# Four edits to a decoder layer on one Trainium2 core: an earlier sample softmax, an on-chip sample output, sooner sample queries and another order of heads in a projection

## The chip, the core and the metric

The kernel runs on one core of a Trainium2 chip. The metric is the device time of one execution in microseconds (us); lower is better. TensorE (PE in the profile) does the matrix products and the transposes, VectorE (DVE) and ScalarE (ACT) do the element-wise work, GpSimd (POOL) a little of it, and SyncE (SP) mostly issues DMA transfers; ACT and POOL issue some transfers too. Each engine works through its own list of instructions in order. The order is fixed when the program is built, so an instruction that waits holds back everything behind it on its engine.

## The reference, cut to what matters

One layer is computed for 1,024 prompt tokens and for 8 sample sequences of 4 new tokens each, 1,056 columns in all, with a model width of 1,024:

```python
SEQ = 1024; DEC_BATCH = 8; DEC_SEQ = 4; PAST_LEN = 512; N_MEM = 256; CA_HEADS = 4
# 1. one input projection -> [S5 diagonal state-space group | differential attention], one output projection
#    prompt: attention over the prompt; sample: over a paged cache of 512 tokens and its own 4
# 2. cross-attention, 4 heads of width 256, into 256 memory tokens
#    (prompt: keys from mem_prompt; sample: cache_mem_k, cache_mem_v, one set for each sequence)
# 3. gated FFN with a causal depthwise convolution
out = g * jax.nn.sigmoid(g @ p['ssm_glu_w'])          # gate behind the state-space scan
s = jnp.einsum('bqhid,bkhid->bhiqk', q, k) * ATTN_HEAD_DIM ** -0.5
pr = jax.nn.softmax(s + bias, axis=-1)
a = pr[:, :, 0] - lam * pr[:, :, 1]                   # differential attention
```

All of it is fp32. Each fp32 product is three products of a high and a low part, so that one tile of a projection takes three matmuls (`mm3`, lines 187 to 189: high by high, low by high, high by low).

## The kernel before

The columns are cut into three blocks, 0 to 383, 384 to 767 and 768 to 1055. The last 32 columns of the third block are the samples. A projection of one 128-wide output tile over one block is 24 matmuls, 8 contraction tiles `k` by three, of 384 or 288 columns. Python generators write the program; a driver takes turns between them by costs that they yield, and a scheduler then settles each engine's order; `tc.high_priority()` ranks what stands in it ahead of other ready work. Four places matter.

**Behind the scan.** The last quarter of the state-space scan (`yp`, `tp__`, gelu on `ge_a` and `yt`) runs beside the sample attention: `soft(s)` turns scores into `Pm` and `Sw`, `values(s)` multiplies pages `V` of the cache by them into `Op`, and the normalized result `os__5850` is transposed into `qsT` by `turn_samples`. The gate products (`zp`, with `th` for the tanh) follow block by block, and the attention result of the prompt comes back from memory as `ms<-mixT`, is split into `Mh` and `Ml` by `load_part`, and feeds the output projection `pp<-Mh`. Sixteen loads of the residual stream (`Xh`, `Xl`) of 528 KB each stand in SP's queue there too; the memory that they fill is free only when the sample attention is done with it.

**Cross-attention.** For each of four heads, three generators run side by side: `wq_head` projects the queries (`pp<-Xh`), `ca_head` does the prompt's attention (scores `S`, probabilities `P`, transposes `pts`, split `Ph`/`Pl`, output `po`), and `sample_keys` does the sample scores. The last loads eight tiles `kt` of 256 KB for a head, through two buffers, has TensorE transpose each (`pt<-ident,kt`), ACT copy it to `KT`, and after every four tiles adds 8 matmuls to `Ssm`. `sample_query` (transposed scale `pb`, then `Qc`) has to come first. All of `pt`, `pts`, `pq` (query norms) and `pb` share two PSUM buffers.

**Output projection of cross-attention.** `wo_stage` takes the heads' outputs from memory (`ms<-coT`, k = 0 to 5) or, for head 3, from SBUF (`coh`, `col`, k = 6 and 7). It does the first four output tiles of blocks 0 and 1, then waits in program order for `sample_values` (16 pages `vt` of 512 KB through three buffers, `Op<-vt`, then `os_`, its transposes `pt<-os_`, and the splits of the sample columns), then does the rest.

**Order of loads.** SP issues `kt`, `ms`, `V` and the weights; POOL issues `vt`.

Of the kernel before, what the change touches and what calls it, by code (L numbers as in the profile page):

```python
# [20 lines left out]
SEQ = 1024  # L21
# [48 lines left out]
def hymba_step(ctx: ExitStack, tc: tile.TileContext, A: dict, O: dict, upto=99, dbg=None):  # L70
# [120 lines left out]
    def fl(a):  # L191
        return a.rearrange("p a b -> p (a b)")
# [1162 lines left out]
    def turn_samples(s, os_, po):  # L1355
        nc.tensor.transpose(po[:, :128], os_, ident)
        nc.vector.tensor_scalar(
            out=qsT[:, :, 16 * s:16 * s + 16].rearrange("p h (b t) -> p b h t", t=DS),
            in0=po[:, :128].rearrange("p (b x) -> p b x", b=4)[:, :, 0:16].rearrange("p b (h t) -> p b h t", t=DS),
            scalar1=gsub, scalar2=None, op0=ALU.mult)  # L1360

    def sample_attention(sa):
# [45 lines left out]

        def soft(s):
            Sp = Sps[s]  # L1410
            Pm = sa.tile([128, PAST + NS], F32, tag="big", name="Pm", bufs=KTB)
            mx = sa.tile([128, 1], F32, tag="mxs", name="mxs")
            sm_ = sa.tile([128, 1], F32, tag="sms", name="sms")
            mx2 = sa.tile([128, 2], F32, tag="mx2", name="mx2")
            c = PAST + NS * s
            nc.vector.tensor_tensor_reduce(out=Pm[:, PAST:], in0=newS[:, s], in1=tabS[:, c:c + NS], scale=-1.0,
                                           scalar=3.0e38, op0=ALU.add, op1=ALU.min, accum_out=mx2[:, 0:1])
            nc.vector.tensor_tensor_reduce(out=Pm[:, :PAST], in0=Sp, in1=tabS[:, :PAST], scale=-1.0,
                                           scalar=3.0e38, op0=ALU.add, op1=ALU.min, accum_out=mx2[:, 1:2])
            tt(out=mx, in0=mx2[:, 0:1], in1=mx2[:, 1:2], op=ALU.min)  # L1420
            nc.scalar.activation(out=Pm, in_=Pm, func=AF.Exp, scale=-1.0, bias=mx, accum_out=sm_)
            nc.vector.reciprocal(out=sm_, in_=sm_)
            tt(out=sm_, in0=sm_, in1=sgn, op=ALU.mult)
            Sw = sa.tile([128, 128], F32, tag="Sw", name="Sw")
            nc.vector.tensor_scalar(out=Sw, in0=fl(Sel), scalar1=sm_, scalar2=None, op0=ALU.mult)
            yield Y[2]
            aT = sa.tile([128, NPG + 1, 128], F32, tag="aT", name="aT")
            pt = tp("pt", "td")
            for pg in range(NPG):
                nc.tensor.matmul(pt[:, 128 * pg:128 * pg + 128], lhsT=Pm[:, 128 * pg:128 * pg + 128], rhs=Sw,  # L1430
                                 start=True, stop=True)
            nc.scalar.copy(fl(aT[:, :NPG]), pt)
            pn = tp("pn", "td")
            nc.tensor.matmul(pn[:NS, :128], lhsT=Pm[:, PAST:], rhs=Sw, start=True, stop=True)
            nc.scalar.copy(aT[:NS, NPG], pn[:NS, :128])
            yield 1100
            aTs.append(aT)
# [99 lines left out]
                                op1=ALU.add)  # L1537
        rsqrt(pl, r, v, 9)

    def load_part(pl, Mh, Ml, src, row, k, b):  # L1540
        t0, n = TB[b]
        ms = pl.tile([128, 384], F32, tag="xn", name="ms", bufs=4)
        nc.sync.dma_start(out=ms[:, :n], in_=src[row:row + 128, t0:t0 + n])
        split(Mh[k][:, t0:t0 + n], Ml[k][:, t0:t0 + n], ms[:, :n])
# [9 lines left out]
    with ExitStack() as p4:  # L1554
# [47 lines left out]
        for b in range(3):  # L1602
            for d in range(4):
                if (d, b) not in early:
                    gate(d, b, (0, 1, 2, 3))
            if b == 1:
                turn_samples(1, tail['os'], ps.tile([128, 512], F32, tag="pj", name="po"))
                nc.gpsimd.dma_start(out=mixT[:, SEQ:].rearrange("(h p) t -> p h t", p=128), in_=qsT)
            for h in range(NH):
                load_part(wx, Mh, Ml, mixT, 128 * h, 4 + h, b)  # L1610
        for d in range(KD):
            for i, X in enumerate((Xh, Xl)):
                nc.sync.dma_start(out=r32(X[:, d]), in_=xT_d[i][128 * d:128 * d + 128, :])
# [17 lines left out]
    with ExitStack() as p5:  # L1631
# [7 lines left out]
        Qc = ca.tile([128, 2, NB, 32], F32, name="Qc", bufs=1)  # L1639
        Ssm = ps_q.tile([128, NMEM], F32, name="Ssm")  # L1640
        hq = {}
        queries = set()
        scaled, late = set(), []
        BORD = [2, 0, 1]
        CKB = 1
# [5 lines left out]
        def wq_head(h):  # L1651
# [15 lines left out]
            nc.vector.memset(ssq, 1.0)  # L1667
            rs = ca.tile([128, 9], F32, tag="crs", name="crs")
            hq[h] = (kh, kl, vh, vl, cqt, rs)
            for oi, bi in enumerate(BORD):  # L1670
                t0, n = TB[bi]
                while h >= 1 and blocks[h - 1] < oi:
                    yield None
                ch = ca.tile([128, 2, 384], F32R, tag="ch", name="ch", bufs=4)
                cl = ca.tile([128, 2, 384], F32R, tag="cl", name="cl", bufs=4)
                sqs = []
                for z in range(2):
                    pp = ps_j.tile([128, 384], F32, tag="pj", name="pp")
                    for k in range(KD):
                        mm3(pp[:, :n], w[z][0][:, k], w[z][1][:, k], Xh[:, k, t0:t0 + n], Xl[:, k, t0:t0 + n],  # L1680
                            k == 0, k == KD - 1)
                        if k % 2:
                            yield 6 * n / 2.4
                    if late:
                        late.pop()()
                        yield 350
                    split_g(ch[:, z, :n], cl[:, z, :n], pp[:, :n], GT[:, 124 + z:125 + z])
                    sq = ca.tile([128, 384], F32, tag="csq", name="csq")
                    nc.scalar.activation(out=sq[:, :n], in_=pp[:, :n], func=AF.Square)
                    sqs.append(sq)  # L1690
                tt(out=sqs[0][:, :n], in0=sqs[0][:, :n], in1=sqs[1][:, :n], op=ALU.add)

                cqt[bi] = (ch, cl)
                late.append(lambda bi=bi, t0=t0, sq=sqs[0]: query_scale(h, bi, t0, sq, ssq, rs))
# [26 lines left out]
        def sample_query(h, cqt, rs):  # L1721
# [7 lines left out]
            for z in range(2):  # L1729
                for s in range(2):  # L1730
# [1 line left out]
                    tt(out=Qc[:, z, 4 * s:4 * s + 4, c:c + 4],  # L1732
                       in0=cs_[:, z, 16 * s:16 * s + 16].rearrange("p (b t) -> p b t", t=DS),
                       in1=pb[:, 16 * s:16 * s + 16].rearrange("p (b t) -> p b t", t=DS), op=ALU.mult)
            queries.add(h)

        def ca_head(h):
            while h not in hq:
# [28 lines left out]
            for oi, bi in enumerate(BORD):  # L1767
# [12 lines left out]
                    split(Ph[:, :, 128 * j:128 * j + 128], Pl[:, :, 128 * j:128 * j + 128], pts)  # L1780
                    yield 220
                yield CA[1]
                if bi == 2:
                    sample_query(h, cqt, rs)
                for z in range(2):
                    po = ps_o.tile([128, 384], F32, tag="po", name="po")
                    for c in range(2):
# [12 lines left out]
                    yield 6 * nq / 2.4  # L1800

        def sample_keys(h):
            while h not in queries:
                yield None
            for s in range(2):
                KT = ca.tile([128, 4, 2, NMEM], F32, tag="KT", name="KT", bufs=CKB)
                for b4 in range(4):
# [53 lines left out]
    with ExitStack() as p7:  # L1861
# [59 lines left out]
        def wo_stage():  # L1921
# [5 lines left out]
            def part(d, b):  # L1927
                t0, n = TB[b]
                pp = ps.tile([128, 384], F32, tag="pj", name="pp")
                for k in range(KD):  # L1930
                    mm3(pp[:, :n], w[d][0][:, k], w[d][1][:, k], Mh[k][:, t0:t0 + n], Ml[k][:, t0:t0 + n],
                        k == 0, k == KD - 1)
                    if k == 3:
                        yield 12 * n / 2.4
                update_x(wx, pp[:, :n], d, t0, n, d == 0)
                yield 12 * n / 2.4
# [197 lines left out]
```

## Time and profile before

| | |
|---|---|
| median of 3 runs | 1818.07 us (1816.73 to 1818.88) |
| the profiled execution | 1823.91 us, span of its instructions 1822.0 us |
| TensorE busy | 1713.6 us, 94% of the span |
| VectorE, ScalarE, GpSimd busy | 60%, 33%, 28% |
| granted TensorE clock, mean | 0.961 |

The profiled execution took 5.84 us more than the median and 1.91 us more than its own span. TensorE is the engine that is nearly always busy; its granted clock is told as a share of full speed, 1.00 at 2.4 GHz and 0.50 at 1.2 GHz. From about 1100 us on, in the FFN, TensorE shows no idle time at clock 1.00, so what can change lies before.

### The profile page before, as it was taken

The numbers are of one execution on the slowest core, as the hardware profiler recorded it, in microseconds if no ns is written. First come the engines' busy times: TensorE is split into PE (matmuls) and PEld (weight loads), VectorE is DVE, ScalarE is ACT, GpSimd is POOL, SyncE is SP. The second block draws the span as 40 slices with busy tenths as digits, with TensorE's granted clock in tenths as the row PEclk, the third lists the DMA queues.
The fourth block names the chain that finished last, engine by engine and source line by source line (L and its number), as shares of the span: only waits on it lengthen the run. The fifth ranks groups of instructions, "written<-read, shape, count | busy, mean of one in ns | idle before, by whom it ended". The sixth has DMA issues, their size and how long they took to land.

```text
span 1822.0 us, 28691 instructions
## 1 busy us (share of the span) xinstructions
PE 1713.6 (94%) x11121; PEld 1596.7 (88%) x11121; DVE 1088.7 (60%) x2563; ACT 602.8 (33%) x1368; POOL 509.3 (28%) x597
## 2 busy tenths in 40 slices
PE   8679999989797899999899999999999999999998
PEld 7458788767685899999769999999999999999997
DVE  6867635666587586555546654654654565555653
ACT  6535335566355343444433211210210211111112
POOL 4456675130300043000033332322312312322210
PEclk9878999989898999999989999999999999999999
DMA  6512232155785722323272111210211211202202
GB/s 174 217 49 80 89 87 91 40 178 172 213 270 163 263 59 64 102 91 94 84 239 70 39 40 31 70 43 28 58 48 35 58 37 46 59 25 58 58 13 97
DMA packets 151809, 170.02 MB, mean 93 GB/s; under 512 B 9528, under 2 KB 125396, under 8 KB 151675
## 3 DMA queue, kind: packets, MB, share of 16 engines
q1 hardware_dynamic: 129650, 114.04, 20.6%
q0 software_dynamic: 10944, 31.95, 5.8%
q10 hardware_dynamic: 11080, 22.21, 3.3%
q8 instruction: 87, 1.43, 0.3%
q14 instruction: 48, 0.39, 0.1%
HBM read 131.86 MB, written 36.30 MB: 92 GB/s over the span
## 4 chain that ended last, share of the span: by engine, by line
PE 79%; DVE 8%; ACT 4%; DMA 3%; issue 1%; SPq 1%; ACTq 0%; POOL 0%; DVEq 0%; POOLq 0%
PE pp L187 5%; PE pp L188 5%; PE pp L189 5%; PE pv L189 5%; PE pv L187 5%; PE pv L188 5%; PE pd L189 5%; PE pd L188 5%; PE pd L187 5%; PE pg L187 5%; PE pg L188 5%; PE pg L189 4%; PE pj L187 2%; PE S L694 2%; PE pj L189 2%; PE pj L188 2%
## 5 line engine op out<-in xcount | busy, mean ns | idle before, releaser
L56 DVE TENSOR_TENSOR xacc<-xacc,pd 128x384 f32<-128x384 f32 (+1 forms) x264 | 135.1, 518 | 169.9 <-PE pd L189 169.9
L56 ACT CAST whi<-raw 128x1024 fp32r<-128x1024 f32 x74 | 77.4, 1049 | 434.0 <-PE pg L188 332.1
L187 PE MATMUL pv<-Xh,whi 128*128 128x384 f32 (+1 forms) x528 | 172.0, 326 | 0.0
L189 PE MATMUL pv<-Xh,wlo 128*128 128x384 f32 (+1 forms) x528 | 171.7, 326 | 0.0
L188 PE MATMUL pv<-Xl,whi 128*128 128x384 f32 (+1 forms) x528 | 171.6, 325 | 0.0
L187 PE MATMUL pd<-ah,dhi 128*128 128x384 f32 (+1 forms) x528 | 171.2, 325 | 0.1
L187 PE MATMUL pg<-Xh,whi 128*128 128x384 f32 (+1 forms) x528 | 171.2, 324 | 0.0
L189 PE MATMUL pd<-ah,dlo 128*128 128x384 f32 (+1 forms) x528 | 170.9, 324 | 0.0
L188 PE MATMUL pd<-al,dhi 128*128 128x384 f32 (+1 forms) x528 | 170.1, 322 | 0.5 <-DVE al L56 0.5
L188 PE MATMUL pg<-Xl,whi 128*128 128x384 f32 (+1 forms) x528 | 170.6, 323 | 0.0
L189 PE MATMUL pg<-Xh,wlo 128*128 128x384 f32 (+1 forms) x528 | 170.1, 322 | 0.0
L56 DVE TENSOR_TENSOR wlo<-raw,whi 128x1024 fp32r<-128x1024 f32 x74 | 108.8, 1471 | 27.7 <-ACT whi L56 21.5
L799 POOL TENSOR_TENSOR raw<-raw,GT 128x1024 f32<-128x1024 f32 x30 | 69.3, 2311 | 158.8 <-DMA raw<-in_ffn_wg_dram 99.4
L187 PE MATMUL pp<-Mh,whi 128*128 128x384 f32 (+1 forms) x336 | 108.9, 329 | 2.5 <-ACT Mh L56 2.5
L187 PE MATMUL pj<-whi,Xh 128*128 128x384 f32 (+1 forms) x288 | 103.0, 360 | 8.0 <-DVE vt L56 7.5
L188 PE MATMUL pp<-Ml,whi 128*128 128x384 f32 (+1 forms) x336 | 109.6, 328 | 0.0
L189 PE MATMUL pp<-Mh,wlo 128*128 128x384 f32 (+1 forms) x336 | 109.5, 327 | 0.0
L188 PE MATMUL pj<-wlo,Xh 128*128 128x384 f32 (+1 forms) x288 | 100.5, 350 | 6.3 <-DVE wlo L56 6.3
L189 PE MATMUL pj<-whi,Xl 128*128 128x384 f32 (+1 forms) x288 | 100.8, 350 | 0.0
L189 PEld LDWEIGHTS pv<-Xh,wlo 128*128 128x128 f32 x528 | 100.0, 189 | 0.1
L187 PEld LDWEIGHTS pv<-Xh,whi 128*128 128x128 f32 x528 | 100.0, 189 | 0.0
L188 PEld LDWEIGHTS pd<-al,dhi 128*128 128x128 f32 x528 | 99.2, 188 | 0.8 <-DVE al L56 0.8
(788 smaller groups left out, 4508.8 us busy)
## 6 DMA issues: line engine op xcount, KB each, us to landing
raw<-in_ffn_wg_dram SPq DMA_DIRECT2D x22, 512.0 KB, 3.9
raw<-in_ffn_wv_dram SPq DMA_DIRECT2D x22, 512.0 KB, 3.9
raw<-in_ffn_wd_dram SPq DMA_DIRECT2D x22, 512.0 KB, 3.8
pg<-in_cache_k_dram SPq DMA_DIRECT2D x32, 256.0 KB, 3.3
V<-in_cache_v_dram SPq DMA_DIRECT2D x32, 256.0 KB, 4.1
kt<-in_cache_mem_k_dram SPq DMA_DIRECT2D x32, 256.0 KB, 3.0
vt<-in_cache_mem_v_dram POOLq DMA_DIRECT2D x16, 512.0 KB, 5.2
raw<-in_w_in_dram SPq DMA_DIRECT2D x48, 128.0 KB, 3.4
```

What stands on the lines that cost most here:

```text
L56: return f(*a, **k)
L187: nc.tensor.matmul(out, lhsT=wh, rhs=xh, start=start, stop=False)
L188: nc.tensor.matmul(out, lhsT=wh, rhs=xl, start=False, stop=False)
L189: nc.tensor.matmul(out, lhsT=wl, rhs=xh, start=False, stop=stop)
L694: nc.tensor.matmul(S[:, i, :w], lhsT=qT[pr, 128 * t:128 * t + 128], rhs=kT[pr, c0:c1], start=True, stop=True, tile_position=(64 * i, 0))
L799: nc.gpsimd.tensor_tensor(out=raw, in0=raw, in1=g.unsqueeze(2).to_broadcast([128, KD, 128]), op=ALU.mult)
```

## The change

It has four parts. The sample softmax of `soft(s)` gets a buffer of its own for `Pm` (before it took one of the two of `KT` and `V`) and is ranked ahead. The last sample output no longer goes to `mixT` in memory and back: `load_part` stops at column 1024, `turn_samples` stands behind all gates, and the sample columns of `Mh` and `Ml` are split from `qsT`. The sample queries are formed at the head of `sample_keys` instead of in `ca_head`, and `wq_head` of the next head waits for them. In `wo_stage` the contraction begins with k = 6 and 7.

```diff
         def soft(s):
-            Pm = sa.tile([128, PAST + NS], F32, tag="big", name="Pm", bufs=KTB)
+            Pm = sa.tile([128, PAST + NS], F32, tag="Pm", name="Pm")
...
+            with tc.high_priority():
+                c = PAST + NS * s
...
+                Sw = sa.tile([128, 128], F32, tag="Sw", name="Sw")
+                nc.vector.tensor_scalar(out=Sw, in0=fl(Sel), scalar1=sm_, scalar2=None, op0=ALU.mult)
...
-    def load_part(pl, Mh, Ml, src, row, k, b):
+    def load_part(pl, Mh, Ml, src, row, k, b, end=NT):
         t0, n = TB[b]
+        n = min(n, end - t0)
...
-            if b == 1:
-                turn_samples(1, tail['os'], ps.tile([128, 512], F32, tag="pj", name="po"))
-                nc.gpsimd.dma_start(out=mixT[:, SEQ:].rearrange("(h p) t -> p h t", p=128), in_=qsT)
             for h in range(NH):
-                load_part(wx, Mh, Ml, mixT, 128 * h, 4 + h, b)
+                load_part(wx, Mh, Ml, mixT, 128 * h, 4 + h, b, SEQ)
+        turn_samples(1, tail['os'], ps.tile([128, 512], F32, tag="pj", name="po"))
+        for h in range(NH):
+            split(Mh[4 + h][:, SEQ:], Ml[4 + h][:, SEQ:], qsT[:, h])
...
-        queries = set()
+        queries, asked = {}, set()
...
+            queries[h] = (cqt, rs)
...
-                while h >= 1 and blocks[h - 1] < oi:
+                while h >= 1 and (blocks[h - 1] < oi or oi and h - 1 not in asked):
                     yield None
...
-            queries.add(h)
+            asked.add(h)
...
-                if bi == 2:
-                    sample_query(h, cqt, rs)
...
         def sample_keys(h):
-            while h not in queries:
+            while (h, 2) not in scaled:
                 yield None
+            sample_query(h, *queries.pop(h))
...
-                for k in range(KD):
+                for i, k in enumerate((6, 7, 0, 1, 2, 3, 4, 5)):
                     mm3(pp[:, :n], w[d][0][:, k], w[d][1][:, k], Mh[k][:, t0:t0 + n], Ml[k][:, t0:t0 + n],
-                        k == 0, k == KD - 1)
-                    if k == 3:
+                        i == 0, i == KD - 1)
+                    if i == 3:
                         yield 12 * n / 2.4
```

Since the scheduler settles the order, the rows of the two programs show what moves. The first place is TensorE in cross-attention, the sample keys of head 1 (`pt_8616` is the transpose of its third tile, `kt_8614`; the second, `pt_8592`, stands 7 matmuls ahead). The changed program reads there:

```order
L1816 MATMUL pt_8592<-ident_71,kt_8590 128x128 x4
...
L1816 MATMUL pt_8616<-ident_71,kt_8614 128x128 x4
L1816 MATMUL pt_8645<-ident_71,kt_8643 128x128 x4
L1782 MATMUL pts_8674<-ident_71,P_8639 128x128 x2
L1822 MATMUL Ssm_7836<-KT_8560,Qc_7835 32x256 x8
L1816 MATMUL pt_8716<-ident_71,kt_8714 128x128 x4
L1816 MATMUL pt_8730<-ident_71,kt_8728 128x128 x4
L1706 MATMUL pq_8736<-ones_76,csq_8571 128x1 x3
L1816 MATMUL pt_8783<-ident_71,kt_8781 128x128 x4
L1782 MATMUL pts_8789<-ident_71,P_8670 128x128 x2
L187 MATMUL pp_8989<-Xh_6563,whi_8886 128x288
```

The program before has the same tiles of head 1 in this order, with stretches of `pp`, `S` and `po` (the `...`) between them:

```order
L1814 MATMUL pt_8795<-ident_71,kt_8793 128x128 x4
L1779 MATMUL pts_8844<-ident_71,P_8692 128x128 x2
...
L1814 MATMUL pt_8872<-ident_71,kt_8870 128x128 x4
L1779 MATMUL pts_8878<-ident_71,P_8789 128x128 x2
L1820 MATMUL Ssm_7829<-KT_8737,Qc_7828 32x256 x8
...
L1814 MATMUL pt_8962<-ident_71,kt_8960 128x128 x4
...
L1814 MATMUL pt_8986<-ident_71,kt_8984 128x128 x4
L1814 MATMUL pt_9024<-ident_71,kt_9022 128x128 x4
```

Tiles three to seven of a head have moved together, with no projection or score between them; before, 21 matmuls of `pp` and `S` stand between the third and the fourth and 18 or more behind the fifth. Heads 2 and 3 look alike in the changed program; in head 0 only tiles five to seven stand together. At the change from one head's last block to the next, the rows `pts` x4, one `po`, `pq`, five `po` of before have become `pts` x2, `pq`, one `po`, 24 `pp`, five `po`.

The second place is TensorE at the end of the first part of the output projection, with the last value pages `vt`. Before:

```order
L1893 MATMUL Op<-vt,PT 32x256 x4
L187 MATMUL pp<-Mh_10220,whi 128x384
...
L189 MATMUL pp<-coh_7807,wlo 128x384
L1907 MATMUL pt<-ident,os__10629 128x128 x2
L187 MATMUL pp<-Mh_10217,whi 128x288 x4
```

In the changed program:

```order
L1895 MATMUL Op<-vt,PT 32x256 x4
L189 MATMUL pp<-Mh_10228,wlo 128x384
L187 MATMUL pp<-Mh_10229,whi 128x384
L188 MATMUL pp<-Ml_10235,whi 128x384
L1895 MATMUL Op<-vt,PT 32x256 x4
L189 MATMUL pp<-Mh_10229,wlo 128x384
L1895 MATMUL Op<-vt,PT 32x256 x12
L1909 MATMUL pt<-ident,os__10636 128x128 x2
L187 MATMUL pp<-coh_7813,whi 128x288 x4
```

Before, 15 projection matmuls stand between the last page and the transposes of `os_`, and 9 between the last two pages. Now the last three pages (x12 is three pages of 4 instructions) and the transposes stand directly behind one another, behind all 192 matmuls of blocks 0 and 1; 17 matmuls stand between pages 11 and 12 of 16, 3 between 12 and 13, 1 between 13 and 14. The projection of the third block, which starts with k = 6 (`coh`), comes next.

The third place is SP's queue behind the last loads of `V`. Before, then now:

```order
L1374 DMA V<-in_cache_v_dram 128x512
L1543 DMA ms<-mixT 128x384 x8
L1613 DMA Xh<-xT_h 128x1056
L1613 DMA Xl<-xT_l 128x1056
```

```order
L1374 DMA V<-in_cache_v_dram 128x512
L1615 DMA Xh<-xT_h 128x1056
L1615 DMA Xl<-xT_l 128x1056
...
L1545 DMA ms<-mixT 128x384 x4
L797 DMA raw<-in_w_out_dram 128x8x128
L1545 DMA ms<-mixT 128x384 x4
```

All sixteen loads of `Xh` and `Xl` now stand ahead of the loads of `ms`. On TensorE the transpose `po<-os__5850` has moved from ahead of the 48 gate products of the third block to behind them, and on DVE the short chain that ends in `os__5850` stands directly behind the last gelu instead of between the gates.

## Rows read from the trace of the kernel before

**Rows 1.** The page's head and busy times: busy us, share of span, instructions.

```profile
span 1822.0 us, 28691 instructions
PE 1713.6 (94%) x11121; PEld 1596.7 (88%) x11121; DVE 1088.7 (60%) x2563; ACT 602.8 (33%) x1368; POOL 509.3 (28%) x597
```

**Rows 2.** Windows of PE: stretch, length, busy (instructions), clock, DMA share, GB/s.

```profile
774.00:784.00 10.00, 8.90 (x54) 0.83 0.24 76
822.00:832.00 10.00, 8.95 (x54) 0.83 0.28 86
870.00:880.00 10.00, 8.96 (x54) 0.83 0.25 79
880.00:896.00 16.00, 13.11 (x86) 0.89 0.32 96
896.00:912.00 16.00, 13.06 (x101) 1.00 0.21 61
912.00:924.00 12.00, 9.64 (x40) 0.57 0.93 304
```

**Rows 3.** Timeline of PE at a head's change: start, us, instruction [idle before, releaser].

```profile
776.73 0.44 PE L187 MATMUL po<-Ph,cvh 128*128 128x384 f32 x1 [0.52 <-ACT Ph L56]
777.75 0.76 PE L1703 MATMUL pq<-ones,csq 128*128 128x1 f32 x6 [0.59 <-DVE Pl L56]
...
780.61 0.52 PE L188 MATMUL pp<-Xl,whi 128*128 128x384 f32 x1
780.93 0.52 PE L189 MATMUL pp<-Xh,wlo 128*128 128x384 f32 x1
...
783.25 0.34 PE L188 MATMUL pp<-Xl,whi 128*128 128x384 f32 x1
783.43 0.33 PE L189 MATMUL pp<-Xh,wlo 128*128 128x384 f32 x1
```

**Rows 4.** Timeline of PE, the first three tiles of head 3's sample keys.

```profile
887.39 0.63 PE L1814 MATMUL pt<-ident,kt 128*128 128x128 f32 x4 [0.19 <-issue]
...
888.45 0.60 PE L1814 MATMUL pt<-ident,kt 128*128 128x128 f32 x4
890.95 0.63 PE L1814 MATMUL pt<-ident,kt 128*128 128x128 f32 x4 [1.90 <-DMA kt<-in_cache_mem_k_dram]
```

**Rows 5.** The tile kt: time from issue to landing of its 32 loads.

```profile
DMA to landing us min/median/max: 2.7/3.0/3.4
```

**Rows 6.** Timeline of PE, a fourth tile and the sample scores behind it.

```profile
805.01 0.60 PE L1814 MATMUL pt<-ident,kt 128*128 128x128 f32 x4
...
806.41 1.07 PE L1820 MATMUL Ssm<-KT,Qc 128*32 128x256 f32 x16 [0.58 <-ACT KT L56]
```

**Rows 7.** Timeline of PE and POOL, the last value pages of the output projection.

```profile
951.36 0.64 PE L1893 MATMUL Op<-vt,PT 128*32 128x256 f32 x8
...
961.95 0.64 PE L1893 MATMUL Op<-vt,PT 128*32 128x256 f32 x8
965.26 0.38 PE L1907 MATMUL pt<-ident,os__10629 128*128 128x128 f32 x2
966.59 0.80 PE L187 MATMUL pp<-Mh,whi 128*128 128x288 f32 x4 [0.94 <-ACT Mh L56]
...
952.32 0.75 POOL L1884 DMA_DIRECT2D vt<-in_cache_mem_v_dram  x1 [3.53 <-PE Op L1893]
```

**Rows 8.** DMA issues between 945 and 960: queue, KB each, us to landing.

```profile
vt<-in_cache_mem_v_dram POOLq DMA_DIRECT2D x4, 512.0 KB, 5.2
```

**Rows 9.** Timeline behind the scan (DVE, SP, PE), and one window of PE.

```profile
578.14 1.47 DVE L56 SCALAR_TENSOR_TENSOR yt<-ge_a,yt 128x512 f32<-128x512 f32 x2
606.72 0.32 SPq L1613 DMA_DIRECT2D Xh<-xT_h  x1
606.74 0.44 PE L1356 MATMUL po<-ident,os__5850 128*128 128x128 f32 x1 [5.39 <-DVE os__5850 L56]
...
606.00:630.00 24.00, 23.26 (x134) 0.87 0.99 372
```

More of the change, by code (lines that the diff above doesn't have):

```diff
@@ L1414, in soft @@
             mx2 = sa.tile([128, 2], F32, tag="mx2", name="mx2")
[L1415 to L1425, printed above, removed]
+            with tc.high_priority():
+                c = PAST + NS * s
+                nc.vector.tensor_tensor_reduce(out=Pm[:, PAST:], in0=newS[:, s], in1=tabS[:, c:c + NS], scale=-1.0,
+                                               scalar=3.0e38, op0=ALU.add, op1=ALU.min, accum_out=mx2[:, 0:1])
+                nc.vector.tensor_tensor_reduce(out=Pm[:, :PAST], in0=Sp, in1=tabS[:, :PAST], scale=-1.0,
+                                               scalar=3.0e38, op0=ALU.add, op1=ALU.min, accum_out=mx2[:, 1:2])
+                tt(out=mx, in0=mx2[:, 0:1], in1=mx2[:, 1:2], op=ALU.min)
+                nc.scalar.activation(out=Pm, in_=Pm, func=AF.Exp, scale=-1.0, bias=mx, accum_out=sm_)
+                nc.vector.reciprocal(out=sm_, in_=sm_)
+                tt(out=sm_, in0=sm_, in1=sgn, op=ALU.mult)
+                Sw = sa.tile([128, 128], F32, tag="Sw", name="Sw")
+                nc.vector.tensor_scalar(out=Sw, in0=fl(Sel), scalar1=sm_, scalar2=None, op0=ALU.mult)
             yield Y[2]
```

## The prediction

> **What bounds the kernel now.** Start with the page's totals: TensorE is busy for 1713.6 of 1822.0 us [rows 1]. So the question is what the other 108 us are, and which of them the change touches. The windows answer it [rows 2]: each line gives the length of a stretch, the busy part of it and the granted clock. Two losses are to be seen. One is idle time (16.00 less 13.11). The other hides in the busy time: where the clock is 0.83 over 10 us, it stood at its lower level, 1.2 GHz, for about (1 - 0.83) x 2 x 10 = 3.4 us. The timeline gives the price of that: matmuls of 384 columns follow each other at 0.32 us there and at 0.18 afterwards [rows 3], so 45% of such time is lost. I therefore price every place twice: what TensorE waits, and what the clock costs afterwards.
>
> **Behind the scan.** TensorE waited 5.39 us for `os__5850` with 48 gate products of 288 columns still to do, and SP's first load of `Xh` went out at the same moment, 606.72 [rows 9]. In the new order the chain to `os__5850` (ten instructions of DVE and a square of ACT) follows the last gelu directly, whose last instructions end at 579.6; at about 0.3 us a step it ends near 583, 24 us sooner. The transposes now stand behind the gates, so that wait goes. What is late next are the loads of `ms`: they queue on SP behind sixteen transfers of 528 KB. These 8.4 MB and what goes beside them took from 607 to about 630 at 372 GB/s [rows 9], so they end near 583 + 22.5 = 605.5. ACT's in-order list has casts of those `ms` ahead of a tanh that TensorE's fourth gate product of the third block needs, so I let TensorE stand from about 600.5 to 607.5. It then has 12 products left where it had 48: 36 x 0.13 (288 columns, three quarters of 0.18) = 4.7 us gained, 0.8 of it lost to the later restart, 0.4 left for loads of `V` that share the transfers. **-3.5 us**, with bounds of -8 (the stall doesn't come) and +1 (the transfers slip by 4 us). The earlier softmax only feeds this chain and is not counted again. The transfer of `qsT` on POOL and its 32 columns read back are not on TensorE's path; I count nothing, since POOL and SP wait there for others.
>
> **Changes of head.** At 774 and 822, TensorE waits for `Ph` and then for `Pl` [rows 3], 1.1 us in each window of 10, and then runs 3.4 us at the lower clock, a loss of 1.5 [rows 2]. In the new order `pq` fills the wait for `Ph`, and 24 projections the wait for `Pl`. Two of these go: **-5.2 us**. The third, at 870, is counted with head 3.
>
> **The sample keys.** This is where I expect the loss. Tiles pass through two buffers, so tile n+2 can be loaded only when tile n is transposed. The trace shows the round trip once, bare: head 3's first tile is transposed at 887.39, the third at 890.95, after 1.90 us of waiting for its transfer [rows 4]. That is 3.56 us from start to start; the landing alone takes 2.7 to 3.4 [rows 5], so it can't be much under 3.2. Before, it was hidden by the projections between the tiles. Now the tiles stand together. The second thing needed is the fourth tile's way through ACT to `Ssm`: 806.41 - 805.01 = 1.40 us [rows 6].
>
> Take head 1, with 0 at the start of its second tile (a tile takes 0.40, `pts` 0.28, `Ssm` 1.0, `pq` 0.7). The third starts at 1.35 after seven matmuls, without a wait. The fourth needs 3.56 and could start at 1.75: 1.8 idle. `Ssm` needs 3.56 + 1.40 = 4.96 and could start at 4.24: 0.7 idle. The fifth follows at 5.96. The sixth needs 7.12 and could start at 6.36: 0.8 idle. The seventh needs 5.96 + 3.56 = 9.52 and could start at 8.22: 1.3 idle. Together 4.6 us of idle in 10. Then the clock: the two waits at 776 were followed by 3.4 us at the lower level [rows 2, 3], here there are four and longer ones, and 23 projections follow; with 3.4 to 5 us of it beyond the pack I take 1.75. So 6.3 us for head 1, and the same for head 2, whose rows are alike: **+12.6 us**. Head 0 has only tiles five to seven together, 0.3 + 0.7 idle by the same round trip, and a clock loss of 1.5: **+2.5 us**.
>
> The Trainium skill bears on this twice. [...] "TensorE: Matmul & The Clock Gate", section on HAM oscillation, says that a loop whose matmuls between two transfers are shorter than the wait for the next one falls to the lower clock each time round. The packs are such loops; the trace agrees at 890.95, behind which the clock of the window falls to 0.89.
>
> **Head 3 and the start of the output projection.** From 870 to 924 TensorE idled 1.04 + 2.89 + 2.94 + 2.36 = 9.2 us [rows 2], and ran 3.4, 3.5 and 10.3 us at the lower clock; 45% of the first two is 3.1, and of the third, in which pages and waits don't suffer, I take 3.0. That makes 15.3 us to be had. In the new order the sample softmax comes sooner and the projection starts with head 3's columns, which never left the chip, so the waits for `ms` and `vt` at its start go, but for about 1. Against that stands the same pack as above with an eighth tile, about 5 us idle; the last two blocks' own softmax waits, which nothing covers, about 4; and a clock loss of about 4. 14 against 15.3: **-1.3 us**, -7 to +5.
>
> **End of the output projection's first part.** A page's buffer comes back 0.96 us (page at 951.36, issue at 952.32) plus 5.2 of landing after the page that held it [rows 7, 8]: 6.2 us. A page's product takes 0.57. In the new order the last page's buffer is freed by page 13, and between them stand one projection and two pages, 0.57 + 0.17 + 1.14 = 1.9 us. So TensorE waits 4.2 us there in two or three parts. Then comes the chain over `os_`, the transposes and the splits: 966.59 - 961.95 = 4.64 us [rows 7]. Before, 15 projections covered it and 0.94 was left; now only its own page and transposes do (0.95), which leaves 3.7. Idle grows by 4.2 + 3.7 - 0.9 = 7.0, and the clock behind it costs 1.7: **+8.7 us**, with bounds of 4.5 (pages landed in time) and 12. That k = 6 comes first in this block means only that the fourth split is waited for instead of the first.
>
> **Sum.** -3.5 - 5.2 + 12.6 + 2.5 - 1.3 + 8.7 = +13.8 us on the profiled 1823.91. That run was 5.84 above the median; I move the median by the same amount, 1818.07 + 13.8 = 1831.9.
>
> **Rivals.** *The tiles are in time, and the kernel is faster.* This would be if the scheduler's order met loads that come back within about 2.3 us. Then the idle of the packs (1.0, twice 4.6, 5) and their clock losses (1.5, twice 1.75, 1.5) go, 21.7 us: 13.8 - 21.7 = -7.9, 1810.2. Against it stands the shortest landing of 2.7 [rows 5]; for it, that only one bare round trip is in the trace. At about 2.9 us the packs would just eat up the gains. *The clock holds.* Between 896 and 912 TensorE idled 2.94 of 16 us at clock 1.00 [rows 2], so sparse work alone doesn't always bring it down. Without the clock losses of the packs and of the end (1.5 + 3.5 + 1.5 + 1.7) the sum is +5.6: 1823.7. *The clock stays down longer.* From 606 to 630 the clock of 0.87 makes 6.2 us of it [rows 9], in the window at 912 it was 10.3. With some 2 us more at four places the sum is +20 or so: 1838. That is also where the Trainium skill's rule on oscillation points if the packs merge into one slow stretch. *The transfers of `Xh` slip or the gain there is double:* +4.5 or -4.5 on the sum, 1836 or 1827. *The waits only change places*, and the sum is within 3.6 us of zero: the packs cost half, 1819.
>
> **Numbers.** A chance of 0.40 for the sum as it stands (1824 to 1839), 0.10 for tiles in time, 0.18 for a clock that holds, 0.14 for one that stays down, 0.10 for the transfers, 0.08 for waits that only change places. A difference of 0.2% (3.6 us) is about what a measurement of this kernel can tell from none. Faster than 1814.4: 0.12, the first rival and a little of the last; within 0.2%: 0.11; slower: 0.77. The range of 1819 to 1841 leaves out the first rival and the far end of the slow clock.
>
> **What would show it.** In the changed profile: waits of 0.7 to 1.9 us of TensorE for `kt<-in_cache_mem_k` and `KT` in heads 1 and 2, about 4.6 in each; no waits for `Ph` and `Pl` at the changes of head; a wait of 3 us or more for `vt` and one of 3 to 4 for `coh` behind the last pages; no 5.39 for `os__5850`, but a stall of some 7 us in the gates of the third block. If the time is under 1820 and the waits for `kt` aren't there, the round trip was mis-read; if they are there and the time is under 1820 all the same, the clock was.

## The result, and the profile after

The changed kernel takes **1842.07 us** (median of 4 runs, 1838.44 to 1846.27) against 1818.18 of the kernel before (4 runs, 1816.73 to 1818.88). The ratio is 1.0121 with a 95% interval of 1.0097 to 1.0145: slower by 24 us by the medians and by 22 by the ratio. The prediction, 1832, had the sign; the median lies 1 us above its range of 1819 to 1841, and 1818.18 times the ratio, 1840.2, just inside it. Two executions that took far longer than all others of their kernel (4618 us of e10, the one that was profiled, and 2122 of the kernel before beside it) are left out of the ratios of this document, and e10 is told by its times alone.

The profiled execution took 1846.27 us, 4 above its median, as that of before was 6 above its own. The page's head and busy times, beside [rows 1]:

```profile
span 1844.5 us, 28682 instructions
PE 1714.8 (93%) x11121; PEld 1597.7 (87%) x11121; DVE 1080.3 (59%) x2567; ACT 603.2 (33%) x1372; POOL 506.8 (27%) x596
```

TensorE does the same 11,121 matmuls in nearly the same busy time, so most of the loss is idle time. Windows of PE (stretch, length, busy with instructions, four more engines, clock, DMA share, GB/s) show where:

```profile
598.00:609.00 11.00, 0.68 (x5) 0.45 (x4) 2.78 (x5) 2.17 (x5) 0.00 (x0) 0.73 1.00 364
609.00:614.00 5.00, 5.00 (x21) 4.98 (x22) 4.76 (x13) 3.86 (x10) 0.00 (x0) 0.56 0.31 89
780.00:790.00 10.00, 9.66 (x62) 9.15 (x62) 7.61 (x31) 5.10 (x12) 0.00 (x0) 1.00 0.24 70
790.00:806.00 16.00, 12.46 (x92) 10.96 (x91) 5.80 (x24) 7.08 (x16) 0.00 (x0) 0.89 0.57 179
842.00:858.00 16.00, 12.61 (x94) 11.14 (x93) 6.62 (x26) 7.23 (x17) 0.00 (x0) 0.89 0.49 157
893.00:930.00 37.00, 26.29 (x148) 20.25 (x147) 16.47 (x69) 12.91 (x35) 0.81 (x1) 0.78 0.29 92
972.00:992.00 20.00, 10.36 (x65) 5.72 (x64) 8.96 (x25) 4.24 (x16) 6.46 (x7) 0.66 0.26 79
```

The first two lines are the gates behind the scan, the third a change of head, the fourth and fifth the sample keys of heads 1 and 2, the sixth head 3, the last the end of the output projection's first part. Only the change of head is better than [rows 2]: 0.34 us idle at clock 1.00 where it was 1.10 at 0.83.

Distances on the two timelines put numbers on the stretches. Between the same two changes of head TensorE does the same instructions in both kernels (144 `pp`, 48 `S`, 36 `po`), so the lengths can be compared. Two marks are less exact. Ahead of the first change stand 24 `pq` matmuls now and 18 before (0.8 us more). Behind the last `pts` of head 3 stand 16 `Ssm`, two transposes of `sP` and 12 `po` before, and six `po` now.

| stretch of TensorE's timeline, us | before | after | more | predicted |
|---|---|---|---|---|
| last matmul into `pjm` to first `pp<-Xh` (gates) | 156.1 | 158.4 | +2.4 | -3.5 |
| to `po` at the first change of head | 67.3 | 74.3 | +7.0 | +2.5 |
| to the second change | 48.7 | 51.4 | +2.7 | +3.7 |
| to the third | 48.0 | 51.2 | +3.3 | +3.7 |
| to the last `pts` of head 3 | 32.9 | 42.4 | +9.5 | |
| to the first `pp` of the third block | 60.3 | 62.7 | +2.4 | |
| to the FFN | 60.5 | 62.2 | +1.7 | +7.4 with the two above |
| sum | 473.7 | 502.6 | +28.9 | +13.8 |

Ahead of the first line the profiled execution of after was 5.4 us quicker and behind the last 1.0, which gives the 22.5 us between the spans. Of the 28.9, 21.9 are idle time of TensorE and 7.0 busy time, which grows where the clock is low. The 5.4 is scatter between executions: that matmul starts between 547.8 and 554.9 us in the thirteen profiles used here, and at 554.32 in a kernel that has all four parts. Single executions differ by some us, so the 28.9 of this pair and the 24 between the medians needn't agree closer than that.

**The gates.** Timeline of PE, ACT, DVE and SP there, beside [rows 9]:

```profile
608.80 0.61 PE L187 MATMUL zp<-Mh,whi 128*128 128x288 f32 x1 [10.32 <-ACT th L56]
...
611.85 0.41 PE L1356 MATMUL po<-ident,os__5850 128*128 128x128 f32 x1
...
606.78 1.58 ACT L56 CAST Mh<-ms 128x384 fp32r<-128x384 f32 x3 [8.93 <-DMA ms<-mixT]
608.27 0.48 ACT L56 ACTIVATE th<-zp 128x384 f32<-128x384 f32 x1
...
574.77 0.35 DVE L56 TENSOR_SCALAR os__5850<-Op,hmask 128x128 f32<-128x128 f32 x1 [3.31 <-PE Op L1454]
...
581.11 0.33 SPq L1615 DMA_DIRECT2D Xh<-xT_h  x1
...
597.07 4.22 SPq L1545 DMA_DIRECT2D ms<-mixT  x4
```

Read it from its last two lines: SP's first `Xh` leaves at 581.11, the first `ms` only at 597.07, behind all sixteen. ACT waits for it until 606.78 and does three of its casts before the tanh `th`, and TensorE has stood for 10.32 us. The 5.39 us for `os__5850` are gone. The line of DVE stands ahead of the last gelu: DVE waits 3.31 us there for the sample product `Op`, and the last gelu ends 31.0 us behind the last matmul into `pjm`, where it ended 26.2 behind it before.

**The sample keys of head 1.** First the tiles on PE's timeline, then the chain of waits of the same stretch (start, us, what):

```profile
791.88 0.60 PE L1816 MATMUL pt<-ident,kt 128*128 128x128 f32 x4
...
793.87 0.63 PE L1816 MATMUL pt<-ident,kt 128*128 128x128 f32 x4 [0.42 <-DMA kt<-in_cache_mem_k_dram]
795.36 0.63 PE L1816 MATMUL pt<-ident,kt 128*128 128x128 f32 x4 [0.86 <-DMA kt<-in_cache_mem_k_dram]
...
796.75 1.07 PE L1822 MATMUL Ssm<-KT,Qc 128*32 128x256 f32 x16 [0.55 <-ACT KT L56]
797.88 0.63 PE L1816 MATMUL pt<-ident,kt 128*128 128x128 f32 x4
799.74 0.63 PE L1816 MATMUL pt<-ident,kt 128*128 128x128 f32 x4 [1.22 <-DMA kt<-in_cache_mem_k_dram]
...
801.36 1.09 PE L1816 MATMUL pt<-ident,kt 128*128 128x128 f32 x4 [0.43 <-DMA kt<-in_cache_mem_k_dram]
```

```profile
792.51 2.71 DMA kt<-in_cache_mem_k_dram
795.22 0.14 issue
795.36 0.64 PE pt L1816 x4
796.00 0.02 issue
796.02 0.59 ACT KT L56
796.61 0.14 issue
796.75 1.07 PE Ssm L1822 x16
797.82 0.06 issue
797.88 0.64 PE pt L1816 x4
798.52 0.02 issue
798.54 2.68 DMA kt<-in_cache_mem_k_dram
```

The second tile starts at 791.88, the fourth, which uses its buffer, at 795.36: a round trip of 3.48 us, most of it the 2.71 of the transfer. The same holds from the fifth to the seventh, 801.36 - 797.88 = 3.48. The chain goes from transfer to transpose to copy to scores and into the next transfer; before, the chain over the eight tiles of head 1 (795.7 to 820.1 us) held no transfer, only matmuls and 1.1 us of ACT.

**Head 0** lost more than its tiles. The fourth and the sixth tile on PE's timeline, SP's queue, and a line of the chain of waits:

```profile
741.70 0.60 PE L1816 MATMUL pt<-ident,kt 128*128 128x128 f32 x4
...
748.44 0.63 PE L1816 MATMUL pt<-ident,kt 128*128 128x128 f32 x4 [3.23 <-DMA kt<-in_cache_mem_k_dram]
...
743.12 0.37 SPq L797 DMA_DIRECT2D raw<-in_ca_wq_dram  x1
743.61 1.02 SPq L1811 DMA_DIRECT2D kt<-in_cache_mem_k_dram  x2
```

```profile
743.61 4.69 DMA kt<-in_cache_mem_k_dram
```

The fourth tile has given its buffer free at 742.3. The sixth's load leaves at 743.61, behind a load of the next head's weights, and takes 4.69 us with the weights' transfer under way.

**The end of the output projection's first part**, beside [rows 7]:

```profile
972.49 0.64 PE L1895 MATMUL Op<-vt,PT 128*32 128x256 f32 x8
...
974.36 0.45 PE L189 MATMUL pp<-Mh,wlo 128*128 128x384 f32 x1
978.82 1.08 PE L1895 MATMUL Op<-vt,PT 128*32 128x256 f32 x8 [4.02 <-DMA vt<-in_cache_mem_v_dram]
981.93 1.08 PE L1895 MATMUL Op<-vt,PT 128*32 128x256 f32 x8 [2.03 <-DMA vt<-in_cache_mem_v_dram]
983.39 1.08 PE L1895 MATMUL Op<-vt,PT 128*32 128x256 f32 x8 [0.38 <-DMA vt<-in_cache_mem_v_dram]
986.63 0.69 PE L1909 MATMUL pt<-ident,os__10636 128*128 128x128 f32 x2 [2.17 <-DVE os__10636 L56]
988.38 1.33 PE L187 MATMUL pp<-coh,whi 128*128 128x288 f32 x4 [1.05 <-ACT coh L56]
...
972.57 2.29 POOL L1528 TENSOR_TENSOR sqa<-sqa,sqx 128x384 f32<-128x384 f32 x2 [5.17 <-ACT sqx L56]
974.81 0.77 POOL L1886 DMA_DIRECT2D vt<-in_cache_mem_v_dram  x1
```

The row at 974.36 is the last product of blocks 0 and 1. The last one before:

```profile
965.09 0.34 PE L189 MATMUL pp<-coh,wlo 128*128 128x384 f32 x1
```

From there to the first product of the third block it took 1.5 us before [rows 7] and takes 14.0 now. TensorE waits 6.43 us for the last three pages and 3.22 for the chain behind them. When the page at 972.49 gave its buffer free, POOL had just begun 2.29 us of sums of squares (`sqa`), and it issued the next load only behind them.

### The profile page after: what moved, and what is told of

It reads as the page before. It is cut to its first block, busy times and chain, and to the rows that moved or that the text cites. A ratio compares the mean times of both kernels' runs of the same rounds, so it can differ in the third digit from the quotient of the medians.

```text
span 1844.5 us, 28682 instructions
## 1 busy us (share of the span) xinstructions
PE 1714.8 (93%) x11121; PEld 1597.7 (87%) x11121; DVE 1080.3 (59%) x2567; ACT 603.2 (33%) x1372; POOL 506.8 (27%) x596
## 4 chain that ended last, share of the span: by engine, by line
PE 77%; DVE 8%; DMA 5%; ACT 5%; issue 1%; POOL 0%; SPq 0%; ACTq 0%; DVEq 0%; POOLq 0%
PE pp L187 5%; PE pp L188 5%; PE pp L189 5%; PE pv L187 5%; PE pv L189 5%; PE pv L188 5%; PE pd L189 5%; PE pd L188 5%; PE pd L187 5%; PE pg L187 4%; PE pg L188 4%; PE pg L189 4%; PE pj L187 2%; PE pj L189 1%; PE pj L188 1%; PE S L694 1%
## 5 line engine op out<-in xcount | busy, mean ns | idle before, releaser
L187 PEld LDWEIGHTS pd<-ah,dhi 128*128 128x128 f32 x528 | 99.0, 188 | 0.9 <-ACT ah L56 0.5
```

Source lines behind the costliest of these rows:

```text
L187: nc.tensor.matmul(out, lhsT=wh, rhs=xh, start=start, stop=False)
```

## The experiments

The theory: the third part alone makes the loss, because its tiles stand together and two buffers come back only after about 3.5 us; the first costs a stall in SP's queue; the fourth moves idle time from the start of the output projection to its end. Rivals: the sooner queries cost time however the tiles stand; the parts lose only together; each repair only moves the idle time. Medians in us, with the median of the kernel before on the same chip:

| kernel | this | before | ratio, 95% interval |
|---|---|---|---|
| e1: first part alone | 1821.53 | 1820.37 | 1.0011, 0.9998 to 1.0025 |
| e2: second alone | 1814.03 | 1820.37 | 0.9972, 0.9952 to 0.9992 |
| e3: third alone | 1841.72 | 1820.37 | 1.0120, 1.0079 to 1.0161 |
| e4: fourth alone | 1817.52 | 1820.37 | 0.9993, 0.9978 to 1.0008 |
| e5: third, two loads a head | 1824.08 | 1818.60 | 1.0039, 1.0025 to 1.0053 |
| e6: second and fourth | 1814.87 | 1818.60 | 0.9978, 0.9956 to 1.0000 |
| e7: first and second | 1823.54 | 1818.60 | 1.0022, 1.0000 to 1.0044 |
| e8: e7, `ms` on POOL's queue | 1819.70 | 1818.60 | 1.0000, 0.9980 to 1.0021 |
| e9: all four, tiles spread | 1825.31 | 1820.90 | 1.0030, 1.0008 to 1.0053 |
| e10: all but the third | 1820.32 | 1820.90 | 1.0000, 0.9981 to 1.0018 |
| e11: e10, `ms` on POOL's queue | 1815.92 | 1820.90 | 0.9981, 0.9965 to 0.9998 |
| e12: e9, `ms` on POOL's queue | 1819.60 | 1819.30 | 0.9997, 0.9974 to 1.0019 |

### e1 to e4: one part at a time

e1, the sample softmax alone:

```diff
-            Pm = sa.tile([128, PAST + NS], F32, tag="big", name="Pm", bufs=KTB)
+            Pm = sa.tile([128, PAST + NS], F32, tag="Pm", name="Pm")
...
+            with tc.high_priority():
```

> The kernel before with the first edit alone (the sample softmax has its own buffer and is ranked ahead). In its order SP's loads of Xh stand ahead of ms, as in the changed kernel. Theory (places priced from the checkpoints of the two traces, where the changed kernel reached cross-attention 3.05 us sooner): this edit brings the gain behind the scan, 1 to 5 us faster, with a stall of TensorE for th of 5 to 10 us in place of the 5.39 us for os__5850. Rival: the gain is the second edit's, and this one is within 1 us of before.

It gains nothing, where 1 to 5 us were expected, and PE's timeline has the stall of the gates already:

```profile
613.14 0.61 PE L187 MATMUL zp<-Mh,whi 128*128 128x288 f32 x1 [10.77 <-ACT th L56]
```

So the first part, not the on-chip output, puts `Xh` and `Xl` ahead of `ms`.

e2, the last sample output on chip alone:

```diff
...
-            if b == 1:
-                turn_samples(1, tail['os'], ps.tile([128, 512], F32, tag="pj", name="po"))
...
-                load_part(wx, Mh, Ml, mixT, 128 * h, 4 + h, b)
+                load_part(wx, Mh, Ml, mixT, 128 * h, 4 + h, b, SEQ)
+        turn_samples(1, tail['os'], ps.tile([128, 512], F32, tag="pj", name="po"))
+        for h in range(NH):
+            split(Mh[4 + h][:, SEQ:], Ml[4 + h][:, SEQ:], qsT[:, h])
```

> The kernel before with the second edit alone (the last sample output stays on chip, its transposes stand behind the gates). Theory: the wait of 5.39 us for os__5850 is filled by the 48 gate products, and the loads of Xh start no later: 2 to 5 us faster. Rival: the wait only moves behind the gates and the time is within 1.5 us of before.

This is the one part that gains, 0.28% or about 5 us. The transposes of `os__5850` follow at 604.18 without a wait, seven of the first eight `ms` leave SP ahead of the first `Xh`, and cross-attention begins 150.1 us after `pjm` where it was 156.1.

e3, the sample queries alone:

```diff
...
-                while h >= 1 and blocks[h - 1] < oi:
+                while h >= 1 and (blocks[h - 1] < oi or oi and h - 1 not in asked):
...
-                if bi == 2:
-                    sample_query(h, cqt, rs)
...
-            while h not in queries:
+            while (h, 2) not in scaled:
                 yield None
+            sample_query(h, *queries.pop(h))
```

> The kernel before with the third edit alone (sample queries formed sooner). In its order the kt tiles of each head stand packed as in the changed kernel. Theory: the packs cost what lies between the checkpoints of the two traces in cross-attention, 7.0 + 2.7 + 3.3 us for heads 0 to 2 and 0 to 3 for head 3: 12 to 17 us slower. Rival (the clock and the end of the output projection carry the loss, the packs' waits are covered): under 6 us slower.

1.0120 alone, 1.0121 with the other three: this part alone loses as much as all four, and more than was expected of it. From the start of cross-attention to the last `pts` it takes 219.8 us, where the kernel before takes 196.8. Eight waits for `kt` of 0.80 to 2.87 us add up to 12.8.

e4, head 3 first in the projection, alone:

```diff
-                for k in range(KD):
+                for i, k in enumerate((6, 7, 0, 1, 2, 3, 4, 5)):
```

> The kernel before with the fourth edit alone (contraction begins with k = 6 and 7). In its order the last three value pages and the transposes of os_ stand directly behind one another, as in the changed kernel. Theory: the end costs 10 to 12 us, the start of the output projection gives back 2 to 5: 5 to 10 us slower. Rival (pages land in time, only the chain over os_ is bare): 0 to 3 us slower.

No difference, where a loss of 5 to 10 us was expected. The windows of the start and of the end of the projection's first part show why:

```profile
903.00:923.00 20.00, 19.45 (x125) 16.53 (x125) 6.69 (x16) 5.39 (x12) 4.55 (x6) 1.00 0.81 260
946.00:964.00 18.00, 10.89 (x71) 7.78 (x70) 6.39 (x21) 2.93 (x12) 4.33 (x6) 0.72 0.26 88
```

In the kernel before the start lost 2.36 us idle in 12 us at clock 0.57 [rows 2]; now it loses 0.55 in 20 at 1.00. At the end 7.1 us are idle instead (1.36, 1.01 and 1.51 for `vt`, 2.17 for `os_`, 1.05 for `coh`). The idle time was moved, and with it the slow clock.

### e5 to e8: what each loss hangs on

e5, the third part with two loads for a head:

```diff
...
-                    kt = ca.tile([128, 2, 256], F32, tag="kt", name="kt", bufs=2)
-                    nc.sync.dma_start(out=kt, in_=A['cache_mem_k'][0, 4 * s + b4, :, h, :]...
+                    if 4 * s + b4 < 2:
+                        kt = ca.tile([128, 2, 256], F32, tag="kt", name="kt", bufs=2)
+                        nc.sync.dma_start(out=kt, in_=A['cache_mem_k'][0, 4 * s + b4, :, h, :]...
+                        kts.append(kt)
+                    kt = kts[b4 % 2]
```

> The third edit alone, as in the run of the queries alone, but of the eight kt tiles of a head only the first two are loaded, and each is transposed four times; the sample scores of the other six sequences are left out in that way. TensorE's order and work stay the same but for a few rows, and no tile waits for a round trip through its buffer. That run took 22 us more than before; its trace shows 13 us of waits for kt in the four heads. Theory (the round trip through two buffers, and the clock behind its waits, carry the loss): these waits and most of the slow-clock time go, 3 to 9 us slower than before. Rival (the packed transposes, copies and softmax waits of head 3 carry it): still over 14 us slower.

With nothing to wait for, the 22 us fall to 7. One window, of e3 and then of e5:

```profile
790.00:806.00 16.00, 11.41 (x85) 9.92 (x84) 5.76 (x23) 7.01 (x16) 0.00 (x0) 0.89 0.49 158
```

```profile
790.00:806.00 16.00, 15.71 (x125) 14.65 (x125) 7.22 (x31) 7.25 (x19) 0.53 (x1) 1.00 0.17 55
```

Idle time and slow clock go together. The transposes, copies and scores are all still there, so it is the loads and their buffers that cost. This run also moves fewer bytes, so it doesn't tell the round trip from the traffic; e9, which keeps every load, does.

e6, the diffs of e2 and e4 together:

> The second and fourth edits together, without the two others. Alone they measured -0.28% and -0.07%. Theory (they work at different places): their sum, 4 to 9 us faster than before. Rival: within 2 us of the second edit alone or worse.

The second part's gain stays and the fourth adds nothing that can be measured.

e7, the diffs of e1 and e2 together:

> The first and second edits together. In this order all loads of Xh stand ahead of ms on SP, as in the changed kernel. Theory (the earlier softmax frees the memory of Xh sooner, the sixteen loads go out ahead of ms, and TensorE stands 10 us for th, which takes back what the second edit gains): within 3 us of before, in the profile a wait of 9 to 11 us for th. Rival (the edits add up): 4 to 8 us faster.

The first part turns a gain of 5 us into a loss of 4. The stall is 10.63 us.

e8, the same with one queue changed:

```diff
-        nc.sync.dma_start(out=ms[:, :n], in_=src[row:row + 128, t0:t0 + n])
+        nc.gpsimd.dma_start(out=ms[:, :n], in_=src[row:row + 128, t0:t0 + n])
```

> The first and second edits together, with the loads of ms issued by POOL instead of SP, so that they don't stand behind the sixteen loads of Xh. Theory (the queue is what holds ms up): the wait for th falls under 4 us, 4 to 10 us faster than before. Rival (the transfers share the same engines, so ms lands hardly sooner): wait for th over 7 us, time within 2 us of the run with the same two edits and ms on SP.

The median fell by 3.8 us from e7, less than expected and no better than before. PE's timeline:

```profile
604.33 0.41 PE L187 MATMUL zp<-Mh,whi 128*128 128x288 f32 x1 [1.67 <-ACT th L56]
...
915.44 1.08 PE L1895 MATMUL Op<-vt,PT 128*32 128x256 f32 x8 [4.57 <-DMA vt<-in_cache_mem_v_dram]
```

The stall of 10.63 is 1.67, and cross-attention begins 150.5 us after `pjm` where e7 has 158.4. But TensorE then stands 4.57 us for the first value page, where it stood 1.45 in e7, and the clock of 905 to 925 us is 0.66 where it was 0.83. That left a question for e11: does the fourth part, which gives TensorE work on the chip just there, keep the gain?

### e9 to e12: the causes taken away

e9, the changed kernel with another cost for a turn:

```diff
                     nc.scalar.copy(KT[:, b4].rearrange("p z m -> p (z m)"), pt.rearrange("p z c m -> p (z c m)"))
-                    yield 440
+                    yield 1040
```

> The changed kernel with all four parts, but a turn of the sample keys costs 1040 where it cost 440, so that projections, scores and values stand between the tiles kt again: by the order of the rows and a round trip of 3.56 us, the waits for kt and KT fall from about 16 us to about 6 (1.7 in head 1, none in head 2, 4.6 in head 3). Theory (the tiles that stand together are the loss): 10 us of waits and about 4 us of clock go, 1842 - 14 = 1828, between 1822 and 1833. Rival (the sooner queries and the held-back projections cost the time themselves, however the tiles stand): 1837 or more.

17 us of the 24 are back with one number, with the sooner queries and all loads in place. The window of e3 and e5 reads here:

```profile
790.00:806.00 16.00, 14.73 (x118) 13.42 (x118) 8.44 (x33) 7.71 (x20) 0.00 (x0) 1.00 0.40 130
```

The waits for `kt` and `KT` over 0.5 us that are left are 1.99, 0.54 and 0.68 us, all in head 3. From the start of cross-attention to the last `pts` it takes 196.9 us, as before (196.8; 219.3 in the changed kernel).

e10, the changed kernel with the diff of e3 undone:

> The changed kernel with the third part undone: sample queries as before, the other three parts kept. Theory (the third part carries the whole loss but the few us by which the softmax takes back the gain of the on-chip output; head 3 first costs at the end what it gains at the start): 1823.5 of the first two parts together, and about nothing for the fourth: 1822, between 1818 and 1827. Rival (the parts add up only together; the third costs less when the others are there): 1830 or more.

1820.32, as the theory had it: without the third part nothing of the loss is left.

e11, the same with the diff of e8:

> The same without the third part, with the loads ms of the gate stage issued by POOL, past the sixteen loads of Xh and Xl in SP's queue. In the run with the first two parts and this queue, the gate stage lost its 10.6 us stall and cross-attention began 7.9 us sooner after the last mixing product, but the first value page vt was then waited for 4.57 us at the start of the output projection. With head 3's columns first there, TensorE has work on the chip until that page lands. Theory: 1822 - 8 = 1814, between 1810 and 1818, with no stall for th over 2 us and none for vt before 930 us. Rival (what the gates gain is always lost at the next transfer, whatever stands there): 1820 or more.

The gain is kept: 4.4 us off e10 and 0.19% faster than the kernel before. The stall for `th` is 1.67 us; one wait of 1.85 for `vt` at 913 is left of the 4.57, so the expectation of none was missed there.

e12, e9 with the diff of e8:

> The changed kernel with all four parts and two repairs: a turn of the sample keys costs 1040, and the loads ms of the gate stage are issued by POOL. Theory (two causes that don't touch each other: tiles that stand together, and ms behind sixteen loads in SP's queue): the spread tiles alone gave 1825, the queue alone took 4.4 us off the kernel without the third part (1820.3 to 1815.9), so 1825 - 4.4 = 1821, between 1817 and 1825, with no stall for th over 2 us and no wait for kt over 0.5 us in heads 0 to 2. Rival (the causes are one, each repair only moves the same idle time on): 1826 or more.

All four parts with the two repairs take as long as the kernel before. Of waits for `kt` over 0.5 us in heads 0 to 2 one of 0.82 is left, where none was expected. The best versions stay e2 (ratio 0.9972), e6 and e11 (0.9978 and 0.9981), which their intervals don't tell apart; the third part is in none of them.

## Why the prediction was right, and where its steps were off

**The sample keys: right, a little too dear.** This step carried the sign. The round trip was read as 3.56 us and is 3.48; the idle time of head 1 is 0.42 + 0.86 + 0.55 + 1.22 + 0.43 = 3.5 and of head 2 3.4 us, where 4.6 was worked out, and the clock stays down for 3.4 us in each, once and not behind each of its waits, which costs 1.5 where 1.75 was taken. So each pack cost about 5.0, not 6.3. e5 and e9 show the cause twice: without the loads, or with work between the tiles, the waits and the slow clock go together. The rival with tiles in time needed loads back within 2.3 us; they take 2.65 to 2.71 in the chain of waits. The Trainium skill ("DMA: Bandwidth & Descriptors", section on the anatomy of one DMA) fits a transfer that GpSimd issues by 2.0 us plus its bytes at 436 GB/s, for 256 KB an estimate of 2.6 us. These loads are SP's, which the fit doesn't speak of; the chain is within about 0.1 of it all the same. What makes the round trip 3.5 is the tile's own 0.6 us and the issue.

**Changes of head: right.** -5.2 was predicted; `po` now waits 0.34 and 0.28 us for `Ph`, nothing waits for `Pl`, and the clock stays at 1.00: about -4.5.

**Head 0: mis-sized, +7.0 for +2.5.** The term took the round trip alone. The sixth tile's load also stood behind a load of weights in SP's queue (1.3 us) and landed only after 4.69 us, where 2.7 was usual: 3.23 us of waiting where 0.3 was counted. Two stretches of 3.2 us at the lower clock cost 1.4 each; one of them was counted (1.5), the other stands behind a wait for `csq` that the kernel before has as well (below). The rest is mostly the six `pq` matmuls that stood behind the mark before (0.8).

**Behind the scan: mis-sized, +2.4 for -3.5, outside its bounds.** What comes late was right: the stall for `th`, 12 products left behind it, no wait for `os__5850`. When was not. The step let TensorE go on 0.8 us later than before (607.5 for 606.7). Counted from the last matmul into `pjm`, it goes on after 60.9 us, where the step has 54.1 and the kernel before 53.4. Half of these 6.7 us is the start: SP's first `Xh` leaves 33.2 us behind that matmul, where 29.6 was worked out from the last gelu of before, and the last gelu now ends 4.8 us later, behind DVE's wait for `Op`. The other half is the stall, 10.32 us for 7: it ends 27.7 us behind the first `Xh` instead of 24.5, since the sixteen transfers and the `ms` behind them took longer. With them the step's sum is +3.2, within 1 us of what was measured. The clock has no part in it: over the whole stretch TensorE is busy for 139.3 us before and 139.0 now. The step also said that the earlier softmax "only feeds this chain". e1, e2 and e7 show that it alone puts the transfers ahead, and that without it the second part gains 5 us.

**Head 3 and the start of the projection: near in the sum, not in its parts, -0.7 for -1.3.** From the third change of head to the last product of blocks 0 and 1 TensorE takes 91.7 us before and 91.0 after. Head 3 loses more than the 3 us that its terms make: it is 5.7 us behind at the first product of the projection. From 893 to 930 us 10.7 us are idle and the clock is 0.78, which is 16 us at the lower level; before, 870 to 912 had 6.9 idle and 6.9 slow [rows 2]. The prediction let the clock there cost 4 against 3.1 gained; the packed tiles and the softmax waits make four slow stretches of 3.4 to 6.9 us, and 9 us more of them cost about 4. The start gives back 6.4 us, the waits and the slow clock of [rows 2]; 1.7 of that is the work of three pages that now come at the end.

**The end of the first part: mis-sized, +14.2 for +8.7.** Between the same two products 12.5 us more go by, and 1.7 more from there to the FFN. 1.7 of it is the work of the three pages. The pages' waits cost 6.4 where 4.2 was counted, since POOL's sums stand ahead of a load in its list, and the chain behind 3.2 where 3.7 was. The clock of 972 to 992 us is 0.66, some 13.6 us at the lower level: the three pages take 1.08 us each instead of 0.64, which comes on top of the 1.7 that was counted. That is the rival of a clock that stays down longer, true in head 3 and here, but not at the gates. e4 shows the fourth part apart: alone, it is worth nothing, where the terms would have made it a loss of some 4 us.

One figure among the rivals, 1819, at which the range begins, is off by its own terms: with half of the packs' 21.7 us gone the sum is about +3 and the time 1821. The measured time is far from either.

The terms that were off by most, the gates (+5.9), the end (+5.5) and head 0 (+4.5), were all too small a loss, and heads 1 and 2 gave back only 1.4; that is how the sign held and the time fell to the upper end of the range.

## What to carry to other kernels

Where transfers come back through few buffers, count what stands between two uses of the same buffer, in the order that the engine really has: here some 3.5 us of other work between tiles n and n+2 hide the load, tiles that stand together cost 22 us (e3), and one number in the interleaving's costs wins 17 of the changed kernel's 24 back (e9). Before a load is let go sooner, look at what it is put ahead of in its queue, and at what the loads behind it release. And a reorder that fills the start of a stage with the work that used to cover its end has gained nothing until the end is looked at too.

## What was not expected of the hardware

The clock doesn't answer equal waits equally. Every kernel here waits for `csq` once, ahead of the second block that head 0 projects, for 2.26 to 2.48 us, with the same work around it. Of thirteen profiled executions the granted clock of the next 4 us was 1.00 in seven and 0.57 to 0.67 in six. PE's window there in the kernel before, and after:

```profile
719.10:723.10 4.00, 4.00 (x23) 4.00 (x24) 1.46 (x4) 0.85 (x3) 0.00 (x0) 1.00 0.23 70
```

```profile
716.05:720.05 4.00, 4.00 (x15) 4.00 (x16) 1.45 (x4) 0.77 (x2) 0.00 (x0) 0.61 0.23 70
```

23 matmuls against 15 in the same time, 1.4 us, for a wait of 2.35 and one of 2.36. The Trainium skill ("TensorE: Matmul & The Clock Gate", section on HAM oscillation) tells of a loop in which each burst of matmuls is shorter than the wait behind it, and whose clock falls each time round. This wait is no such case: TensorE is busy without a gap for the 10 us ahead of it in all thirteen, and the clock fell in about half. What decides it stays open. A clock loss of one place is so worth a chance, not a sum, and a few such places may explain part of the scatter between executions; that was not tested apart.
